# A hybrid decoder step: the sums of squares placed among product groups, w_o's parts spread one to a step, and silu(z) loaded behind a later chunk's operands

## The chip, the core and the metric

The kernel runs on one core of a Trainium2 chip. The core has five engines, each with its own instruction stream that it works through in order: PE (TensorE, the matrix multiplications and transposes), DVE (VectorE), ACT (ScalarE), POOL (GpSimd) and SP (SyncE, which here only issues DMA transfers). Engines wait for each other, and for transfers, by semaphores. An instruction that waits holds up everything behind it on its own engine; this goes for a DMA issue on SP too. Matrix results go to PSUM banks, all else lies in SBUF, and large arrays in the chip's memory. The metric is the device time of one execution in microseconds (us); lower is better.

## What is computed

One layer, for a prompt of 1024 tokens and for 8 samples of 8 tokens, with 1024 model channels; together 1088 columns of work. Cut to what matters here:

```
h = rmsnorm(x) * (1 + scale) + shift
[u_pool | z_pool | z_ssm | xBC | dt | g] = h @ w_in
P = (pool_mix(u_pool) * silu(z_pool)) @ w_pool_out
y = SSD(conv(xBC)) + D * x                      # a scan over chunks of 128 tokens, in 4 groups of 8 heads
S = (rmsnorm(y * silu(z_ssm)) * g) @ w_ssm_out  # the mean of squares runs over all 2048 channels
x = x + gate * ((sigmoid(g_pool) * P + sigmoid(g_ssm) * S) @ w_o)
out = rmsnorm(x)
```

Inside the scan, for each chunk and head: decay matrices `exp(...)` from the cumulated dt, an inner product of C and B weighted with them, the state carried from chunk to chunk, and at the end `v = (y + D x) * silu(z)`. The norm's factor 1/sqrt(mean(v*v)) is the same for all channels of a token, so the kernel multiplies v by w_ssm_out first and applies the factor afterwards. For it the squares of v are summed over the channels in `sq_acc`, 128 partitions by 1088 columns.

## The kernel before, in words

Everything is kept with channels on partitions and tokens along the free axis. Products are made in float32r from a high half (a rounded copy, on ACT) and a low half (the rest, by a subtraction on DVE or POOL), three matrix multiplications for a full product. The program has four stretches: the norm of x and the first projections; the projections with w_in, convolution and pooling; from about 795 us on the scan over chunks with product groups of w_pool_out and w_ssm_out between; and the last group's products, the gates, and the product with w_o.

The change is in the third stretch and at its seam to the fourth.

**The loop over chunks.** There are 32 chunks, 8 to each of the 4 groups. `chunk(g, c)` is a generator; the loop advances several of them in each iteration i, so that the work on chunk i stands beside the preparation of those behind it. Step 1 (called for chunk i+3 in iteration i) issues on SP the loads of `dec` (decays, 512 KB, three buffers), `bc` (128 KB, three buffers) and `xb` (256 KB, five buffers). Step 2 (for chunk i+2) makes the exponentials: POOL masks `dec` (L1294), ACT takes exp (L1298, L1603). Step 3 (chunk i+1) first loads `sz`, the 256 KB of silu(z) (L1609, three buffers), then transposes xb on PE (L1612) and prepares on DVE `xd`, `xw`, `dec`, `cE` (L1623 to L1632). Step 4 (chunk i) does the products of the scan on PE (L1637, L1310, L1313), updates the state `hst` (POOL L1643, DVE L1645) and adds D*x on DVE (L1650). Step 5 is `finish`: DVE multiplies by sz (L1570), ACT takes the high half and the square (L1572, L1573), POOL the low half (L1574, the last use of xb's buffer) and three additions that end in sq_acc (L1575 to L1581, the last use of sz's buffer).

**Product groups as fillers.** `pieces()` yields after each of 96 product groups (12 matrix multiplications into one of three PSUM banks, `mm`, which DVE or ACT then empties, L1831, L1849, L1852). `products(t)` advances it by 2.56 groups an iteration; ten are left after the loop.

**w_o.** `wo_splits()` makes five combinations of the quarters of w_o for a Strassen-like product, each in a high and a low half, and puts them into memory. It takes four passes, for 128 rows of each half of w_o: two loads of 512 KB (`R` from `in_w_o`, three buffers, L1895 and L1896), four operations on DVE (L1902 to L1908), then five parts, each a copy on ACT with its store from ACT's queue (`ph`, three buffers, L1883, L1884), a subtraction on POOL (L1885) and a store on SP (L1890). The loop advances it once an iteration from i = 10 on.

**What sets the order.** PE and SP issue in the order in which the code is written (`in_line`). On ACT, DVE and POOL a scheduler chooses the order when the program is built, so the place of an instruction in the code is not its place on these engines.

**The seam.** After the loop the ten product groups that are left come first. Then sq_acc is split into `sq_h` (ACT L1989) and `sq_l` (POOL L1991, written as `m`), six matrix multiplications with ones sum over the partitions (L1997, L1998), ACT takes the root (L1999) and DVE the reciprocal `rstd` in three pieces (L2000). The last group's products follow: eight units of three groups, each emptied by DVE (L2051), with four more operations of DVE per unit (L2044 with rstd, L2056, L2057, and L2032 or L2036).

Of the kernel before, what the change touches and what calls it, by code (L numbers as in the profile page):

```python
# [46 lines left out]
def tile_pool_ssd_step(  # L47
# [1535 lines left out]
    def sample_end(g):  # L1583
# [4 lines left out]
        yield  # L1588
        finish(g, SEQ, NS, v, sz)

    def chunk(g, c):
        o = c * P
        dec = ckt([P, 8, P], "dec", 3)
        decays(dec, g, c)
        bc = ckt([P, 2, P], "bc", 3)
        load(bc, xbc_d[g][:, 4:6, o:o + P])
        Bf, Cf = bc[:, 0], bc[:, 1]
        xb = ckt([P, 4, P], "xb", 5)
        load(xb, xbc_d[g][:, 0:4, o:o + P])
        yield  # L1600
        if c > 0:
            cE = ckt([P, 8, P], "cE")
            act(cE, dec, AF.Exp, scale=-1.0)  # L1603
        if g > 0 or c > 0:
            far(dec, c)
            exps(dec, g, c)
            yield
        sz = ckt([P, 4, P], "sz", 3)
        load(sz, z_d[g][:, :, o:o + P])  # L1609
        px = PB()  # L1610
        for q in range(4):
            nc.tensor.transpose(px[:, q * P:(q + 1) * P], xb[:, q], ident)  # L1612
# [10 lines left out]
        V.tensor_tensor(xd, pxv, dtT[:, c, heads].unsqueeze(2).to_broadcast([P, 8, 64]), ALU.mult)  # L1623
# [12 lines left out]
        pu = PC()  # L1636
        mm(pu, bt, xw.rearrange("p h d -> p (h d)"), start=True, stop=True)  # L1637
        pi = inner(xd, dec, P, *((hst[g], cE) if c > 0 else ()))
        hn = ckt([P, 512], "hst", 2)
        if c == 0:  # L1640
            act(hn, pu, AF.Copy)
        else:
            nc.gpsimd.tensor_tensor(hn.rearrange("p (h d) -> p h d", d=64), hst[g].rearrange("p (h d) -> p h d", d=64),  # L1643
                                    Elb[:, c, heads].unsqueeze(2).to_broadcast([P, 8, 64]), ALU.mult)
            V.tensor_tensor(hn, hn, pu, ALU.add)  # L1645
        hst[g] = hn

        v = xb
        for q in range(4):
            V.scalar_tensor_tensor(v[:, q], v[:, q], Dv[:, 4 * g + q:4 * g + q + 1], pi[:, q], ALU.mult, ALU.add)  # L1650
        yield
        finish(g, o, P, v, sz)
        if c == NC - 1:
            yield
            pt = PB()
            for q in range(4):
                nc.tensor.transpose(pt[:, q * P:(q + 1) * P], hn[:, q * P:(q + 1) * P], ident)
            fo = ckt([P, 4, P], "xb", 5)
            act(fo, pt.rearrange("p (q n) -> p q n", n=P), AF.Copy)
            store_(new_ssm_p[0, 0, 8 * g:8 * g + 8].rearrange("(q h) p n -> (h p) q n", h=2), fo)  # L1660
# [217 lines left out]
    def wo_splits():  # L1878
# [9 lines left out]
        def out():  # L1888
            while outs:
                load(*outs.pop(0))  # L1890
        left_, right_ = slice(0, 512), slice(512, 1024)

        def rows(k):
            up, dn = R(), R()
            load(up[:, :D], w_o[0, k * P:k * P + P, :])  # L1895
            load(dn[:, :D], w_o[0, 512 + k * P:512 + k * P + P, :])  # L1896
            return up, dn
        got = rows(0)
        yield
        for k in range(4):  # L1900
            up, dn = got
            WOE.tensor_tensor(dn[:, right_], dn[:, right_], up[:, right_], ALU.subtract)  # L1902
            WOE.tensor_tensor(up[:, right_], up[:, right_], up[:, left_], ALU.subtract)
            out()
            yield
            t2 = ckt([P, 512], "t2", 1)
            WOE.tensor_tensor(t2, dn[:, right_], up[:, left_], ALU.add)
            WOE.tensor_tensor(dn[:, left_], t2, dn[:, left_], ALU.subtract)  # L1908
            part(oT1, k, up[:, right_])
            yield  # L1910
            out()
            part(oB11, k, up[:, left_])
            part(oT2, k, t2)
            yield
            out()
            part(oT4, k, dn[:, left_])
            yield
            if k < 3:
                got = rows(k + 1)
            out()  # L1920
            part(oT3, k, dn[:, right_])
            yield
        out()
        yield
    WOE = V
    wos = wo_splits()
    RATE = 2.56
    FRONT = 4

    def products(t):  # L1930

# [9 lines left out]
    for _ in range(FRONT - 1):  # L1941
        next(pc_)
    next(seq[0])
    next(seq[1])
    next(pc_)
    in_line(first_engines)
    order = tuple(mybir.EngineType[e] for e in ORDER)
    for i in range(len(seq)):
        if i + 1 < len(seq):
            next(seq[i + 1])  # L1950
        products(i + 0.4)
        if i > 0:
# [33 lines left out]


    sq_h = mp.tile([P, T], F32R, tag="sq_h", name="sq_h", bufs=1)
    act(sq_h, sq_acc, AF.Copy)  # L1989
    sq_l = M(dt=F32R)  # L1990
    nc.gpsimd.tensor_tensor(sq_l, sq_acc, sq_h.bitcast(F32), ALU.subtract)  # L1991
    ones_r = sm.tile([P, P], F32R, tag="stc", name=nm("ones_r"), bufs=4)
    act(ones_r, ones, AF.Copy)
    rstd = mp.tile([P, T], F32, tag="rstd", name="rstd", bufs=1)
    for o, n in GB:
        ps = PB()
        mm(ps[:, :n], ones_r, sq_h[:, o:o + n], start=True, stop=False)  # L1997
        mm(ps[:, :n], ones_r, sq_l[:, o:o + n], start=False, stop=True)  # L1998
        act(rstd[:, o:o + n], ps[:, :n], AF.Sqrt, bias=eps, scale=1.0 / DI)  # L1999
        V.reciprocal(rstd[:, o:o + n], rstd[:, o:o + n])  # L2000
# [320 lines left out]
```

## Time and profile before

| | |
|---|---|
| median of three runs | 1261.52 us (1261.42 to 1265.95) |
| the profiled execution | 1261.8 us, span of its instructions 1260.1 us |
| granted TensorE clock, mean over the span | 0.995 |
| PE, DVE, POOL, ACT busy | 98%, 77%, 57%, 53% |
| w_o loads, of all passes | 8 of 512 KB, on SP |

A row of the timeline gives start and duration in us, engine, line, operation, `out<-in`, shapes, and in brackets how long the engine was idle before and what ended it. `SPq` is SP issuing a DMA. In the list of waits the numbers are the total in us, how often, and the longest. In the windows they are the stretch, its length, busy time (and instructions) of PE, PE's weight loads, DVE, ACT and POOL, then the granted clock, the DMA share and GB/s. In the chain of waits a row gives start, duration and what the chain went through.

### The profile page before, as it was taken

What the parts mean: (1) busy time and instruction counts of PE and PEld (TensorE: products, weight loads), DVE (VectorE), ACT (ScalarE), POOL (GpSimd) and SP (SyncE); (2) the same over time, 40 slices, a digit from 0 to 9 for tenths busy, and PEclk for the clock granted to TensorE, in tenths of its full rate; (3) what the DMA queues carried; (4) which work ended last, traced back from release to release, by engine and by line L of the source; (5) the groups of instructions that cost most, each with busy time, mean ns of one, the idle gap of its engine ahead of it and who ended that gap; (6) DMA issues with size and microseconds to landing.
All of it is one profiled execution on the core that took longest, in us unless ns stands there. A gap on an engine that the chain in (4) does not pass through costs nothing.

```text
span 1260.1 us, 26422 instructions
## 1 busy us (share of the span) xinstructions
PE 1237.0 (98%) x9703; PEld 1158.3 (92%) x9703; DVE 970.3 (77%) x1685; ACT 673.2 (53%) x1545; POOL 722.6 (57%) x608
## 2 busy tenths in 40 slices
PE   9999999999999999999999999999999989999997
PEld 8889999999999999999999999998898978898885
DVE  6893888877988688886666675687787969679996
ACT  6764366655656566546444444556586646401425
POOL 1137768776968678654433435255677758513663
PEclk9999999999999999999999999999999989999999
DMA  9946455474546554435575665997869868775884
GB/s 317 309 137 212 124 177 178 135 233 129 184 154 202 164 154 159 157 111 152 158 199 162 179 195 171 329 312 256 261 221 312 259 215 259 242 268 186 251 194 157
DMA packets 262715, 257.53 MB, mean 204 GB/s; under 512 B 27993, under 2 KB 202345, under 8 KB 262578
## 3 DMA queue, kind: packets, MB, share of 16 engines
q1 hardware_dynamic: 181856, 163.49, 42.4%
q10 hardware_dynamic: 78426, 88.16, 20.2%
q0 software_dynamic: 2304, 4.20, 1.9%
q8 instruction: 77, 1.26, 0.4%
q14 instruction: 52, 0.43, 0.1%
HBM read 170.80 MB, written 85.10 MB: 203 GB/s over the span
## 4 chain that ended last, share of the span: by engine, by line
PE 62%; DVE 5%; DMA 3%; issue 1%; POOL 1%; ACT 0%; SPq 0%; DVEq 0%; ACTq 0%; POOLq 0%
PE mm L427 14%; PE ps L427 14%; PE mm L235 13%; PE ps L1310 2%; PE pc L427 2%; PE pc L1637 2%; PE ps L1313 2%; PE ps L2118 2%; PE ps L2116 2%; PE ps L2117 2%; DMA R<-in_w_o 1%; PE ps L1402 1%; DMA xb<-xbc 1%; PE ps L1612 1%; PE ps L1425 1%
## 5 line engine op out<-in xcount | busy, mean ns | idle before, releaser
L151 POOL TENSOR_TENSOR wlo<-rawA,whi 128x512 fp32r<-128x512 f32 x120 | 173.1, 1446 | 115.9 <-ACT whi L148 105.6
L151 POOL TENSOR_TENSOR wlo<-raw,whi 128x512 fp32r<-128x512 f32 x90 | 152.8, 1707 | 89.4 <-ACT whi L148 85.3
L235 PE MATMUL mm<-Y,whi 128*128 128x352 f32 (+1 forms) x960 | 198.0, 336 | 2.7 <-DVE G L2051 2.2
L235 PEld LDWEIGHTS mm<-Y,whi 128*128 128x128 f32 x960 | 160.0, 189 | 11.0 <-DVE G L2051 4.9
L1148 DVE SCALAR_TENSOR_TENSOR GA<-GA,cvT,GA 128x1112 f32<-128x1112 f32 x72 | 133.8, 1863 | 0.1
L427 PE MATMUL mm<-Y,whi 128*128 128x272 f32 x800 | 120.1, 292 | 0.0
L148 ACT ACTIVATE whi<-rawA 128x512 fp32r<-128x512 f32 x120 | 75.2, 627 | 82.6 <-PE ps L427 45.6
L427 PE MATMUL ps<-Y,whi 128*128 128x272 f32 x800 | 117.8, 289 | 0.0
L427 PEld LDWEIGHTS mm<-Y,whi 128*128 128x128 f32 x800 | 107.6, 188 | 2.6 <-issue 1.1
L148 ACT ACTIVATE whi<-raw 128x512 fp32r<-128x512 f32 x90 | 55.8, 628 | 100.9 <-DVE raw L364 42.4
L427 PEld LDWEIGHTS ps<-Y,whi 128*128 128x128 f32 x800 | 106.7, 188 | 0.3
L235 PE MATMUL mm<-Y,wlo 128*128 128x352 f32 (+1 forms) x480 | 99.0, 328 | 0.0
L1298 ACT ACTIVATE dec<-dec,acT 128x128 f32<-128x128 f32 x256 | 78.5, 389 | 25.1 <-POOL dec L1294 25.1
L235 PEld LDWEIGHTS mm<-Y,wlo 128*128 128x128 f32 x480 | 82.2, 189 | 0.0
L302 POOL TENSOR_TENSOR pw<-pw,ph 128x512 fp32r<-128x512 f32 x40 | 66.5, 1663 | 10.5 <-ACT ph L300 10.2
L427 PE MATMUL mm<-G,whi 128*128 128x272 f32 x480 | 71.0, 290 | 0.0
L427 PE MATMUL ps<-G,whi 128*128 128x272 f32 x480 | 70.5, 289 | 0.0
L427 PE MATMUL mm<-Y,wlo 128*128 128x272 f32 x400 | 66.7, 288 | 0.0
L427 PE MATMUL ps<-Y,wlo 128*128 128x272 f32 x400 | 66.5, 288 | 0.0
L1574 POOL TENSOR_TENSOR Y<-xb,Y 128x512 fp32r<-128x512 f32 x32 | 41.2, 1290 | 42.0 <-ACT Y L1572 42.0
L427 PEld LDWEIGHTS mm<-G,whi 128*128 128x128 f32 x480 | 64.4, 189 | 0.7
L427 PEld LDWEIGHTS ps<-G,whi 128*128 128x128 f32 x480 | 64.2, 188 | 0.4 <-issue 0.4
(597 smaller groups left out, 3260.0 us busy)
## 6 DMA issues: line engine op xcount, KB each, us to landing
rawA<-in_w_in SPq DMA_DIRECT2D x62, 512.0 KB
dec<-acs_d SPq DMA_DIRECT2D x32, 512.0 KB
xbc<-GA ACTq DMA_DIRECT2D x24, 512.0 KB
Y<-wo SPq DMA_DIRECT2D x10, 1024.0 KB
pw<-in_w_ssm_out ACTq DMA_DIRECT2D x32, 256.0 KB
ws<-ph ACTq DMA_DIRECT2D x32, 256.0 KB
ws<-pw ACTq DMA_DIRECT2D x32, 256.0 KB
h<-in_state_ssm SPq DMA_DIRECT2D x32, 256.0 KB
```

What stands on the lines that cost most here:

```text
L148: ins = act(hi[:, :, :ncols], raw[:, :, :ncols], AF.Copy)
L151: (eng or nc.gpsimd).tensor_tensor(lo[:, :, :ncols], raw[:, :, :ncols], hi[:, :, :ncols].bitcast(F32), ALU.subtract)
L235: mm(ps[:, :n], w[k // 4][h][:, k % 4, :], r[k][:, o:o + n], start=(j == 0), stop=(j == len(terms) - 1))
L302: nc.gpsimd.tensor_tensor(raw.bitcast(F32R), raw, hi.bitcast(F32), ALU.subtract)
L427: mm(p, w[j // 8][:, k], A(k, s)[j // 4 == 1], start=(j == 0), stop=(j == 11))
L1148: V.scalar_tensor_tensor(d[:, :n], rp[:, k:k + n], cvT[:, 24 * k + mc:24 * k + mc + 1], d[:, :n], ALU.mult, ALU.add)
L1298: act(dec[:, h], dec[:, h], AF.Exp, bias=acT[:, c, 8 * g + h:8 * g + h + 1], scale=-1.0)
L1310: mm(o[hh], xd[:S, 2 * q + hh, :], dec[:S, 2 * q + hh], start=True, stop=state is None)
L1313: mm(o[hh], state[:, h * 64:h * 64 + 64], cE[:, h], start=False, stop=True)
L1574: nc.gpsimd.tensor_tensor(yl[g][:, :, o:o + S], v, yhc.bitcast(F32), ALU.subtract)
L1637: mm(pu, bt, xw.rearrange("p h d -> p (h d)"), start=True, stop=True)
L2116: mm(ps, hi, y[:, k, c0:c0 + cw], start=(first and k == 0), stop=False)
```

## The change

Three things are moved; the arithmetic is the same.

- sz is no longer loaded in step 3 of its chunk. `load_sz(j)` loads it, called in iteration i for chunk i+1, after step 1 of chunk i+3.
- `wo_splits()` starts at i = 8 and loads one 512 KB block at a time; each step holds one part at most.
- After the loop only four of the ten product groups come first. sq_h and sq_l are made in three pieces each, sq_l on DVE. Each sum over the partitions is followed by its root, reciprocals of at most 128 columns (nine in all) and one product group; the last three groups come behind.

```diff
+    szs = []
+
+    def load_sz(j):
+        g, c = divmod(j, NC)
+        szs.append(ckt([P, 4, P], "sz", 3))
+        load(szs[-1], z_d[g][:, :, c * P:c * P + P])
+
     def chunk(g, c):
...
-        sz = ckt([P, 4, P], "sz", 3)
-        load(sz, z_d[g][:, :, o:o + P])
         px = PB()
...
-        finish(g, o, P, v, sz)
+        finish(g, o, P, v, szs.pop(0))
...
-        def rows(k):
-            up, dn = R(), R()
-            load(up[:, :D], w_o[0, k * P:k * P + P, :])
-            load(dn[:, :D], w_o[0, 512 + k * P:512 + k * P + P, :])
-            return up, dn
-        got = rows(0)
+        def row(o):
+            t = R()
+            load(t[:, :D], w_o[0, o:o + P, :])
+            return t
+        up, dn = row(0), None
         yield
         for k in range(4):
-            up, dn = got
-            WOE.tensor_tensor(dn[:, right_], dn[:, right_], up[:, right_], ALU.subtract)
-            WOE.tensor_tensor(up[:, right_], up[:, right_], up[:, left_], ALU.subtract)
             out()
+            if k:
+                part(oT3, k - 1, dn[:, right_])
+            old, dn = dn, row(512 + k * P)
+            yield
+            V.tensor_tensor(dn[:, right_], dn[:, right_], up[:, right_], ALU.subtract)
+            V.tensor_tensor(up[:, right_], up[:, right_], up[:, left_], ALU.subtract)
+            out()
+            if k:
+                part(oT4, k - 1, old[:, left_])
             yield
             t2 = ckt([P, 512], "t2", 1)
-            WOE.tensor_tensor(t2, dn[:, right_], up[:, left_], ALU.add)
-            WOE.tensor_tensor(dn[:, left_], t2, dn[:, left_], ALU.subtract)
+            V.tensor_tensor(t2, dn[:, right_], up[:, left_], ALU.add)
+            out()
             part(oT1, k, up[:, right_])
             yield
+            V.tensor_tensor(dn[:, left_], t2, dn[:, left_], ALU.subtract)
             out()
             part(oB11, k, up[:, left_])
-            part(oT2, k, t2)
             yield
             out()
-            part(oT4, k, dn[:, left_])
-            yield
+            part(oT2, k, t2)
             if k < 3:
-                got = rows(k + 1)
-            out()
-            part(oT3, k, dn[:, right_])
+                up = row(k * P + P)
             yield
...
+    BEFORE = 4
...
     next(seq[0])
+    load_sz(0)
     next(seq[1])
...
             next(seq[i + 3])
+        if i + 1 < len(seq):
+            load_sz(i + 1)
         if i + 2 < len(seq):
             next(seq[i + 2])
         next(seq[i], None)
...
-        if i > 9:
+        if i > 7:
             next(wos, None)
         products(i + 1.0)
     next(seq[-1], None)
-    for it in (pc_, wos):
-        for _ in it:
-            pass
-    in_line(order)
+    for _ in wos:
+        pass
+    for _ in range(BEFORE):
+        next(pc_)
...
     sq_h = mp.tile([P, T], F32R, tag="sq_h", name="sq_h", bufs=1)
-    act(sq_h, sq_acc, AF.Copy)
     sq_l = M(dt=F32R)
-    nc.gpsimd.tensor_tensor(sq_l, sq_acc, sq_h.bitcast(F32), ALU.subtract)
...
+    for o, n in GB:
+        s = slice(o, o + n)
+        act(sq_h[:, s], sq_acc[:, s], AF.Copy)
+        V.tensor_tensor(sq_l[:, s], sq_acc[:, s], sq_h[:, s].bitcast(F32), ALU.subtract)
     for o, n in GB:
...
         act(rstd[:, o:o + n], ps[:, :n], AF.Sqrt, bias=eps, scale=1.0 / DI)
-        V.reciprocal(rstd[:, o:o + n], rstd[:, o:o + n])
+        for a in range(o, o + n, P):
+            b = min(a + P, o + n)
+            V.reciprocal(rstd[:, a:b], rstd[:, a:b])
+        next(pc_, None)
+    for _ in pc_:
+        pass
+    in_line(order)
```

The lines behind the change shift by up to 23, so the loop's L1609 is L1596 afterwards, L1885 is L1890, L1902 is L1910 and L2000 is L2019. What the change does to the engines' orders is shown at three places.

SP, from the loads of chunk 25 (the first three rows) to those of chunk 26, before. The sz is that of chunk 24:

```order
L1290 DMA dec_13976<-acs_d 128x1024
L1596 DMA bc_13978<-xbc_173 128x2x128
L1599 DMA xb_13980<-xbc_173 128x4x128
L1609 DMA sz_14021<-z_169 128x4x128
L324 DMA whi_14038<-ws_201 128x512
L325 DMA wlo_14039<-ws_201 128x512
L1290 DMA dec_14082<-acs_d 128x1024
L1596 DMA bc_14084<-xbc_173 128x2x128
L1599 DMA xb_14086<-xbc_173 128x4x128
```

The same stretch now, where sz_13986 is that of chunk 23 and sz_14091 that of chunk 24:

```order
L1290 DMA dec_13980<-acs_d 128x1024
L1603 DMA bc_13982<-xbc_173 128x2x128
L1606 DMA xb_13984<-xbc_173 128x4x128
L1596 DMA sz_13986<-z_168 128x4x128
L1895 DMA wo_11259<-R_13542 128x512
L324 DMA whi_14041<-ws_201 128x512
L325 DMA wlo_14042<-ws_201 128x512
L1290 DMA dec_14085<-acs_d 128x1024
L1603 DMA bc_14087<-xbc_173 128x2x128
L1606 DMA xb_14089<-xbc_173 128x4x128
L1596 DMA sz_14091<-z_169 128x4x128
```

sz of chunk 24 has moved from ahead of chunk 26's three loads to behind them.

DVE in w_o's third pass, before (`R` and `t` are w_o's, `hst`, `xb`, `xd`, `xw`, `dec` and `cE` the chunks', `G<-mm` a product bank being emptied):

```order
L1625 TENSOR_TENSOR xw_13812<-ps_13799,wdT 128x512
L1645 TENSOR_TENSOR hst_13849<-hst_13849,pc_13830 128x512
L1630 TENSOR_TENSOR dec_13614<-dec_13614,ps_13804 128x1024
L1632 TENSOR_TENSOR cE_13743<-cE_13743,ps_13804 128x1024
L1902 TENSOR_TENSOR R_13771<-R_13771,R_13770 128x512
L1650 SCALAR_TENSOR_TENSOR xb_13510<-xb_13510,Dv,ps_13832 128x128 x4
L1852 TENSOR_TENSOR G_12637<-mm_13885,G_12637 128x352
L1903 TENSOR_TENSOR R_13770<-R_13770 128x512
L1907 TENSOR_TENSOR t_2351_14000<-R_13771,R_13770 128x512
```

And now:

```order
L1628 TENSOR_TENSOR xd_13693<-ps_13682,dtT 128x512
L1910 TENSOR_TENSOR R_13648<-R_13648,R_13542 128x512
L1857 TENSOR_TENSOR G_12513<-mm_13699,G_12513 128x352
L1635 TENSOR_TENSOR dec_13509<-dec_13509,ps_13687 128x1024
L1637 TENSOR_TENSOR cE_13623<-cE_13623,ps_13687 128x1024
L1911 TENSOR_TENSOR R_13542<-R_13542 128x512
L1917 TENSOR_TENSOR t_2334_13884<-R_13648,R_13542 128x512
L1630 TENSOR_TENSOR xw_13695<-ps_13682,wdT 128x512
L1650 TENSOR_TENSOR hst_13732<-hst_13732,pc_13713 128x512
```

Before, w_o's operations came behind xw and hst of a chunk; now they come one chunk earlier (chunk 21 in place of 22), and xw and hst stand behind three of them.

POOL in the same pass now (`R` and `t` with `ph` are w_o's five subtractions):

```order
L1294 AFFINE_SELECT dec_13615<-dec_13615 128x1024
L1890 TENSOR_TENSOR R_13542<-R_13542,ph_13887 128x512
L1890 TENSOR_TENSOR R_13542<-R_13542,ph_14008 128x512
L1648 TENSOR_TENSOR hst_13849<-hst_13732,Elb 128x512
L1890 TENSOR_TENSOR t_2334_13884<-t_2334_13884,ph_14114 128x512
L1890 TENSOR_TENSOR R_13648<-R_13648,ph_14239 128x512
L1574 TENSOR_TENSOR Y_13240<-xb_13386,Y_13239 128x4x128
L1575 TENSOR_TENSOR sz_13621<-sz_13621 128x256
L1294 AFFINE_SELECT dec_13739<-dec_13739 128x1024
L1890 TENSOR_TENSOR R_13648<-R_13648,ph_14365 128x512
```

Before, the five stood within eight instructions of POOL, with hst, Y and sz between the third and the fourth; now they stand within nine. The code's steps are one part long, but the order of POOL is the scheduler's.

DVE at the seam, before and now:

```order
L1852 TENSOR_TENSOR G_13216<-mm_15126,G_13216 128x384
L1852 TENSOR_TENSOR G_13216<-mm_15140,G_13216 128x352
L1852 TENSOR_TENSOR G_13216<-mm_15154,G_13216 128x352
L2000 RECIPROCAL rstd<-rstd 128x384
L2000 RECIPROCAL rstd<-rstd 128x352 x2
L2051 TENSOR_TENSOR G_12255<-mm_15223,G_12255 128x384
```

```order
L1857 TENSOR_TENSOR G_12953<-mm_15070,G_12953 128x352
L2019 RECIPROCAL rstd<-rstd 128x128 x3
L1857 TENSOR_TENSOR G_13076<-mm_15109,G_13076 128x384
L2019 RECIPROCAL rstd<-rstd 128x128 x2
L2019 RECIPROCAL rstd<-rstd 128x96
L1857 TENSOR_TENSOR G_13076<-mm_15130,G_13076 128x352
L2019 RECIPROCAL rstd<-rstd 128x128 x2
L2019 RECIPROCAL rstd<-rstd 128x96
L1857 TENSOR_TENSOR G_13076<-mm_15151,G_13076 128x352
L1857 TENSOR_TENSOR G_13216<-mm_15165,G_13216 128x384
L2067 TENSOR_TENSOR R_15228<-rstd,R_15228 128x1088
```

The reciprocals have moved from ahead of the last group's first eviction to between the evictions of the product groups ahead of it.

More of the change, by code (lines that the diff above doesn't have):

```diff
@@ L1891, in wo_splits @@
         left_, right_ = slice(0, 512), slice(512, 1024)
-        def rows(k):
-            up, dn = R(), R()
-            load(up[:, :D], w_o[0, k * P:k * P + P, :])
-            load(dn[:, :D], w_o[0, 512 + k * P:512 + k * P + P, :])
-            return up, dn
-        got = rows(0)
+        def row(o):
[3 more added lines that the diff above has]
+        up, dn = row(0), None
         yield
         for k in range(4):
-            up, dn = got
-            WOE.tensor_tensor(dn[:, right_], dn[:, right_], up[:, right_], ALU.subtract)
-            WOE.tensor_tensor(up[:, right_], up[:, right_], up[:, left_], ALU.subtract)
             out()
+            if k:
[7 more added lines that the diff above has]
+                part(oT4, k - 1, old[:, left_])
             yield
             t2 = ckt([P, 512], "t2", 1)
-            WOE.tensor_tensor(t2, dn[:, right_], up[:, left_], ALU.add)
-            WOE.tensor_tensor(dn[:, left_], t2, dn[:, left_], ALU.subtract)
+            V.tensor_tensor(t2, dn[:, right_], up[:, left_], ALU.add)
+            out()
             part(oT1, k, up[:, right_])
             yield
+            V.tensor_tensor(dn[:, left_], t2, dn[:, left_], ALU.subtract)
             out()
             part(oB11, k, up[:, left_])
-            part(oT2, k, t2)
             yield
             out()
-            part(oT4, k, dn[:, left_])
-            yield
+            part(oT2, k, t2)
             if k < 3:
-                got = rows(k + 1)
-            out()
-            part(oT3, k, dn[:, right_])
+                up = row(k * P + P)
             yield
         out()
+        part(oT3, 3, dn[:, right_])
         yield
-    WOE = V
+        out()
+        part(oT4, 3, dn[:, left_])
+        yield
+        out()
     wos = wo_splits()
```

## The prediction

> **What bounds the kernel now.** I read the page's busy times first, then who waited for whom on PE, then the chain of waits, and last the rows of SP, POOL, DVE and PE around each wait. The page:
>
> ```profile
> PE 1237.0 (98%) x9703; PEld 1158.3 (92%) x9703; DVE 970.3 (77%) x1685; ACT 673.2 (53%) x1545; POOL 722.6 (57%) x608
> ```
>
> PE is busy nearly always, so only its idle and its slow time can be won. The waits of PE, one wait of SP, and three windows tell where these lie:
>
> ```profile
> PE ps L1612 <- DMA xb<-xbc: 5.7, 2, 4.6
> PE mm L235 <- DVE G L2051: 2.2, 3, 1.5
> ...
> PE ps L1313 <- POOL Y L1574: 0.7, 1, 0.7
> ```
> ```profile
> SPq L1609 <- POOL sq_acc L1581: 29.9, 7, 9.0
> ```
> ```profile
> 1000.00:1020.00 20.00, 19.24 (x152) 16.54 (x150) 18.04 (x31) 13.31 (x36) 18.66 (x19) 1.00 0.46 136
> ...
> 1028.00:1030.00 2.00, 1.90 (x9) 1.93 (x10) 0.69 (x1) 0.94 (x4) 1.03 (x1) 0.50 1.11 391
> ```
>
> Two groups of transposes waited for xb, 4.63 and 1.05 us. After the first the granted clock is 0.50 for a while. The chain of waits shows what that cost, beside the same work at full clock:
>
> ```profile
> 1012.13 4.04 PE mm L235 x24
> 1016.17 0.44 PE ps L1612 x4
> ...
> 1020.93 7.04 DMA xb<-xbc
> ...
> 1028.10 1.09 PE ps L1612 x4
> ...
> 1029.83 5.60 PE mm L235 x24
> ```
>
> 24 products took 5.60 in place of 4.04 and four transposes 1.09 in place of 0.44: 2.2 us on top of the 4.63. The large stall costs 6.8 us, the small one 1.05.
>
> Why xb came late: SP's rows, then POOL's.
>
> ```profile
> 1003.21 0.33 SPq L1290 DMA_DIRECT2D dec<-acs_d  x1
> ...
> 1004.07 0.51 SPq L1599 DMA_DIRECT2D xb<-xbc  x1
> 1018.26 0.53 SPq L1609 DMA_DIRECT2D sz<-z  x1
> ...
> 1020.93 0.46 SPq L1599 DMA_DIRECT2D xb<-xbc  x1
> ...
> 1068.49 0.53 SPq L1609 DMA_DIRECT2D sz<-z  x1
> ...
> 1070.21 0.46 SPq L1599 DMA_DIRECT2D xb<-xbc  x1
> ```
> ```profile
> 999.64 0.89 POOL L1581 TENSOR_TENSOR sq_acc<-sq_acc,sz 128x128 f32<-128x128 f32 x1
> ...
> 1002.75 2.99 POOL L1885 TENSOR_TENSOR R<-R,ph 128x512 fp32r<-128x512 f32 x2 [0.72 <-ACT ph L1883]
> ...
> 1009.08 1.27 POOL L1574 TENSOR_TENSOR Y<-xb,Y 128x512 fp32r<-128x512 f32 x1
> ...
> 1017.77 0.88 POOL L1581 TENSOR_TENSOR sq_acc<-sq_acc,sz 128x128 f32<-128x128 f32 x2
> ...
> 1065.60 1.30 POOL L1574 TENSOR_TENSOR Y<-xb,Y 128x512 fp32r<-128x512 f32 x1
> ...
> 1067.99 0.47 POOL L1581 TENSOR_TENSOR sq_acc<-sq_acc,sz 128x128 f32<-128x128 f32 x1
> ```
>
> SP goes in order. (I number the 32 chunks from 0 on through the four groups.) From 1004.6 to 1018.26 it stood at sz of chunk 24, until POOL had added chunk 21 to sq_acc, which is when that buffer of sz comes free; POOL was late there, with w_o's subtractions (L1885) in a bunch before it. Behind this sz stood dec, bc and xb of chunk 26. The same happened with sz of chunk 29 (chunk 26 added at 1068.46) and xb of chunk 31.
>
> **The change, part by part.** *sz behind the loads.* No load is added. Now xb of chunk i+3 stands ahead of sz of chunk i+1; the sz ahead of it is that of chunk i, which needs POOL one chunk less far. For xb 26 that is sz 23, free once chunk 20 was added: 999.64 + 0.89 = 1000.5. What is left for xb is PE, which holds dec's buffer, and POOL's L1574, which holds xb's own. PE's rows:
>
> ```profile
> 1000.44 1.02 PE L1637 MATMUL pc<-xw,bt 128*128 128x512 f32 x2
> ...
> 1008.16 1.02 PE L1637 MATMUL pc<-xw,bt 128*128 128x512 f32 x2
> ...
> 1028.10 1.09 PE L1612 MATMUL ps<-ident,xb 128*128 128x128 f32 x4 [4.63 <-DMA xb<-xbc]
> ...
> 1060.22 1.02 PE L1637 MATMUL pc<-xw,bt 128*128 128x512 f32 x2
> ...
> 1075.95 0.66 PE L1612 MATMUL ps<-ident,xb 128*128 128x128 f32 x4 [1.05 <-DMA xb<-xbc]
> ```
>
> dec is loaded 2.8 us after L1637 (1000.44 and 1003.21), xb 0.9 later. One chunk on, L1637 at 1008.16 gives xb 26 at 1011.9, its L1574 having ended at 1010.35. With the measured 7.04 it lands at 1018.9, and PE wanted it at 1028.10 - 4.63 = 1023.5: covered by 4.6 us. For xb 31, L1637 at 1060.22 gives 1063.9, but its L1574 ends at 1066.9; with 7.04 it lands at 1073.9 and is wanted at 1074.9: covered by 1.0 us. So both stalls go: 6.8 + 1.05 = 7.85 us. Bounds: 0, where another late thing takes their place, and 7.85. What that 0.50 clock makes of a stall that only shrinks is told by a page: the Trainium skill, TensorE: Matmul & The Clock Gate, What's actually happening, says that the clock halves after an idle window of about 3.4 us. The trace agrees (0.50 after 4.63 us, no slower products after 1.05). By that rule a stall left at 2 us would still give back all 2.2 us of slow clock, and the sum would be 2 us worse, not 2.9.
>
> What is late next is sz itself. Chunk 24's could still not go before 1018.26; by xb's 7.04 it lands at 1025.3, and DVE multiplied by it at
>
> ```profile
> 1025.92 0.68 DVE L1570 TENSOR_TENSOR xb<-xb,sz 128x512 f32<-128x512 f32 x1
> ```
>
> so it is just in time in the worst chunk. I take 0; the other end is 2 us, once, if it lands as late as xb's longest wait suggests.
>
> *w_o's parts.* The same eight loads, 16 DVE operations, 20 halves on ACT and POOL and 40 stores; the first load two chunks earlier, one 512 KB block at a time in place of two. In the new program's order POOL's five subtractions of a pass still stand within ten instructions (shown with the change), so the spreading itself I cost at nothing. What can cost is DVE, which waited for w_o before:
>
> ```profile
> DVE R L1902 <- DMA R<-in_w_o: 5.6, 3, 3.8
> ```
> ```profile
> 987.69 7.23 DMA R<-in_w_o
> ```
> ```profile
> L1903 DVE TENSOR_TENSOR R<-R x4: 677/687/1515, 907.8 to 1050.0; 128x512 f32<-128x512 f32 x4
> ```
>
> The second block of a pass is now issued behind sz and one store, about half a us later after its dec than before, and lands 7.2 us after. In the third pass the first subtraction stands right behind xd of chunk 21, and xw of chunk 21 stands behind three of w_o's operations. In this trace these places are
>
> ```profile
> 976.11 0.34 SPq L1290 DMA_DIRECT2D dec<-acs_d  x1
> ```
> ```profile
> 982.78 0.68 DVE L1623 TENSOR_TENSOR xd<-ps,dtT 128x512 f32<-128x512 f32 x1
> ```
> ```profile
> 990.80 1.02 PE L1637 MATMUL pc<-xw,bt 128*128 128x512 f32 x2
> ```
>
> so the block goes at about 976.1 + 2.4 = 978.5 and lands at 985.7; DVE is there at 983.4 and waits 2.3 us. Then seven operations (four of 0.6 to 0.7, two of dec and cE at 1.2, an eviction of 0.5) bring xw to 991.3, 0.5 us after PE wanted it. In the other passes the next consumer on PE stands a chunk further on. I take a loss of 0.5; bounds 0 and 2.4 us in each pass. The rule that speaks against this part is in the Trainium skill, SBUF — State Buffer, Who interferes with whom: a DVE instruction with two SBUF inputs and a POOL instruction that reads SBUF shut each other out for a whole instruction. The 677 to 1515 ns of L1903 agree. By that rule all three operations of w_o ahead of xw would be held, to about 1.5 us each, xw would be 3.0 us late in place of 0.5, and the forecast would stand at 1255.0. The 0.7 us of L1313 is of the same kind; I leave it standing.
>
> *Sums of squares and reciprocals.* The rows at the seam between the loop and the last group's products:
>
> ```profile
> 1097.26 0.56 DVE L1852 TENSOR_TENSOR G<-mm,G 128x384 f32<-128x384 f32 x1 [1.55 <-PE mm L235]
> ...
> 1113.90 6.98 DVE L2000 RECIPROCAL rstd<-rstd 128x384 f32<-128x384 f32 x3 [0.44 <-ACT rstd L1999]
> ...
> 1122.06 3.68 DVE L2044 TENSOR_TENSOR R<-rstd,R 128x1088 f32<-128x1088 f32 x3
> ```
> ```profile
> 1121.34 0.97 PE L235 MATMUL mm<-Y,whi 128*128 128x384 f32 x4 [1.52 <-DVE G L2051]
> ```
>
> From 1093 to 1113 DVE does one eviction of about 0.5 us for each product group of PE, 1.95 us, and is idle in between. Then 6.98 us of reciprocals stand ahead of the evictions, and PE pays 2.2 us in three waits. The change puts 7 us of reciprocals, the 3.7 of L2044 and three subtractions of 0.5 (the low half, now DVE's) beside the same ten product groups. Six of them, 11.7 us, come behind the first sum; their evictions need 3.2, the reciprocals and L2044 10.7: DVE enters the last group about 2.2 us behind instead of 7 and then 3.7. A piece of 128 columns takes a third of the 2.3 to 2.6 us of a reciprocal, 0.85, so no eviction waits long, and PE's lead of three banks, two groups or 3.9 us, hides the rest. The four groups ahead of the first sum last from 1093 to 1100.9, POOL's last addition ends at 1096.4, so ACT's three pieces and DVE's subtractions are covered by 4.5 us. I take 1.7 of the 2.2 us, since L2056 and L2057 keep DVE nearly full behind it; bounds 0 and 2.2.
>
> **Sum.** 7.85 + 1.7 - 0.5 = 9.05 us off the profiled execution's 1261.8: 1252.7. The median of the three runs is 0.3 lower (1261.52); rounded down, 1252.5.
>
> **Rivals.** *DVE stands at w_o's second block (the slower side).* If the longest wait seen, 3.8 us, comes in all four passes and DVE's next three operations take 1.5 in place of 0.68 (+2.5), DVE is 6.3 us late in each. Where a product bank is PE's next need, its lead of 3.9 us leaves 2.4 to pay; where xw is, nothing covers. At a mean of 4.5 us in a pass 18 are lost and 9.55 won: 1270. It decides from 2.4 us a pass on. For it: DVE's 18.04 of 20 us busy from 1000 on. Against it: it waited in three passes before, and PE lost 0.7.
>
> *Another late thing takes half the stall.* POOL was busy 18.66 of those 20 us, DVE 18.04, and the stall let both catch up; without it the next chunk may wait for cE or hst instead. Half of the 6.8 is then kept: about 1256.
>
> *The move of sz does nothing:* POOL's L1574 is so late that xb waits for it as sz did. The 1.0 us of xb 31 speaks for it, the 4.6 of xb 26 against. Only the seam is won: 1260.
>
> **Chances.** My forecast 0.60, half the stall 0.20, only the seam 0.08, slower 0.12. A measurement of this kernel can tell about 0.5%, 6.3 us, from no change, so faster means below 1255.2. The forecast and two fifths of the second case lie there: 0.68 faster, 0.20 within, 0.12 slower. The range goes from 1250, where 7.85 + 0.7 + 2.2 are won, to 1262, which takes in all but the slower case.
>
> **What would show it.** Right: no wait of PE for xb and no clock of 0.50 in the chunk loop; SP's wait for sq_acc still there, with dec and xb issued ahead of it; reciprocals between evictions and no wait of 1.5 us behind them. Wrong: PE waiting for DVE or POOL between two chunks, DVE waiting for w_o more than 3.8 us in a pass, or L1570 waiting for sz.

## The result, and the profile after

The changed kernel takes 1252.68 us (median of 6 executions, 1248.57 to 1254.32). The kernel before, with three more executions beside it, has a median of 1264.58 us (1261.42 to 1265.95). The ratio is 0.9907, 95% interval 0.9886 to 0.9928. The two profiled executions are 7.5 us apart (spans of 1260.1 and 1252.6 us); one state product early and one late cut both into three stretches. Line numbers have moved: the state product is L1637 before and L1642 after, silu(z)'s load L1609 and L1596, xb's load L1599 and L1606. PE's first and last state products in the timeline of the kernel after:

```profile
810.51 1.02 PE L1642 MATMUL pc<-xw,bt 128*128 128x512 f32 x2
...
1083.31 1.02 PE L1642 MATMUL pc<-xw,bt 128*128 128x512 f32 x2
```

Before, these rows began at 809.48 and 1087.74. So the way to the first state product is 1.0 us longer (of the edits only the first loads of silu(z) lie there, and a second execution of the same kernel was 1.1 us shorter there than before), the chunk loop takes 272.8 us in place of 278.3 (5.5 less), and the rest, from the last state product to the end, 169.3 in place of 172.4 (3.1 less). These three lengths are given for every run below; the first varies from 808.1 to 811.2 us among all of them, whatever the edit.

The loop first. SP's rows and POOL's rows for the same chunks as in the prediction:

```profile
1005.72 0.44 SPq L1606 DMA_DIRECT2D xb<-xbc  x1
1008.06 0.52 SPq L1596 DMA_DIRECT2D sz<-z  x1
...
1013.43 0.42 SPq L1606 DMA_DIRECT2D xb<-xbc  x1
1013.94 0.53 SPq L1596 DMA_DIRECT2D sz<-z  x1
```
```profile
1007.57 0.47 POOL L1581 TENSOR_TENSOR sq_acc<-sq_acc,sz 128x128 f32<-128x128 f32 x1
...
1011.49 0.46 POOL L1581 TENSOR_TENSOR sq_acc<-sq_acc,sz 128x128 f32<-128x128 f32 x1
```

The first sz still goes out right behind an addition to sq_acc (1007.57 + 0.47, then 1008.06), but xb stands ahead of it. Where SP stood for 13.7 us before, the longest pause between two of its rows from 950 us on is 7.6 us, and it is not at silu(z). The waits of SP and of PE from 780 us on:

```profile
SPq L1596 <- POOL sq_acc L1581: 12.6, 5, 4.5
```
```profile
PE ps L1310 <- DVE cE L1637: 1.8, 1, 1.8
PE ps L1310 <- ACT dec L1298: 1.2, 1, 1.2
PE ps L1619 <- DMA dec<-acs_d: 0.4, 1, 0.4
PE mm L235 <- DVE Y L1680: 0.3, 1, 0.3
```

No wait for xb is left. In their place stand two waits that the kernel before did not have, 1.8 and 1.2 us. The timelines of DVE, SP, PE and ACT show where they come from:

```profile
1040.77 0.67 DVE L1650 TENSOR_TENSOR hst<-hst,pc 128x512 f32<-128x512 f32 x1
1045.05 1.26 DVE L1570 TENSOR_TENSOR v<-v,szs 128x256 f32<-128x256 f32 x1 [3.61 <-DMA v<-ys]
1046.23 1.21 DVE L1635 TENSOR_TENSOR dec<-dec,ps 128x1024 f32<-128x1024 f32 x1
1047.36 1.21 DVE L1637 TENSOR_TENSOR cE<-cE,ps 128x1024 f32<-128x1024 f32 x1
```
```profile
1037.82 1.49 SPq L1587 DMA_DIRECT2D v<-ys  x1
```
```profile
1048.72 0.44 PE L1310 MATMUL ps<-dec,xd 128*64 128x128 f32 x4 [1.82 <-DVE cE L1637]
...
1058.02 0.44 PE L1310 MATMUL ps<-dec,xd 128*64 128x128 f32 x4 [1.18 <-ACT dec L1298]
```
```profile
1051.42 0.63 ACT L1572 ACTIVATE Y<-xb 128x512 fp32r<-128x512 f32 x1 [2.89 <-DVE xb L1570]
...
1052.98 2.43 ACT L1298 ACTIVATE dec<-dec,acT 128x128 f32<-128x128 f32 x8
```
```profile
1055.52 1.22 DVE L1635 TENSOR_TENSOR dec<-dec,ps 128x1024 f32<-128x1024 f32 x1 [1.48 <-ACT dec L1298]
1056.66 1.21 DVE L1637 TENSOR_TENSOR cE<-cE,ps 128x1024 f32<-128x1024 f32 x1
```

v holds the sample columns of the last group; they are multiplied by their silu(z) (tile szs) once a group. The load goes out at 1037.82 and lands 7.2 us later; DVE reaches the multiplication at 1041.4 and stands 3.6 us, and dec and cE of the next chunk, which PE's next products need, stand behind it. That is the wait of 1.8 us. The second follows from it one chunk on: ACT waited 2.9 us for the late DVE, its exponentials came behind that, and DVE waited 1.5 us for these before its next dec and cE. The profile names ACT for this wait of PE, but PE starts 0.15 us after cE ends, as it did at the first. In the kernel before the same multiplication stood behind dec and cE, and its load had 9.4 us:

```profile
1042.84 0.87 SPq L1587 DMA_DIRECT2D v<-ys  x1
```
```profile
1047.77 1.21 DVE L1630 TENSOR_TENSOR dec<-dec,ps 128x1024 f32<-128x1024 f32 x1
1048.90 1.21 DVE L1632 TENSOR_TENSOR cE<-cE,ps 128x1024 f32<-128x1024 f32 x1
...
1052.27 0.76 DVE L1570 TENSOR_TENSOR v<-v,szs 128x256 f32<-128x256 f32 x1
```

The edit does not touch that multiplication. The scheduler, which orders DVE, put it elsewhere; that it did so because other work had moved is a reading of the orders and was not tested. The stand is 3.1 to 3.9 us in the three executions that have both w_o's edit and the move of sz's load, with v's load where it was. It is 0.7 and 0.8 us in the two that have w_o's edit without sz's move, and absent in the two that have sz's move without w_o's edit.

The seam. DVE's rows after the first sum, and PE's waits from 1083 us on:

```profile
1097.63 2.58 DVE L2019 RECIPROCAL rstd<-rstd 128x128 f32<-128x128 f32 x3 [0.44 <-ACT rstd L2016]
1100.13 0.49 DVE L1857 TENSOR_TENSOR G<-mm,G 128x384 f32<-128x384 f32 x1
1100.54 2.36 DVE L2019 RECIPROCAL rstd<-rstd 128x128 f32<-128x128 f32 x3
...
1106.31 3.69 DVE L2067 TENSOR_TENSOR R<-rstd,R 128x1088 f32<-128x1088 f32 x3
```
```profile
PE mm L235 <- DVE G L2074: 0.9, 1, 0.9
```

The nine reciprocals and the products with rstd lie between evictions, DVE is done with them at 1110, and one wait of 0.9 us in the last group is left of the 2.2.

### The profile page after: what moved, and what is told of

It reads as the page before. It is cut to its first block, busy times and chain, and to the rows that moved or that the text cites. A ratio compares the mean times of both kernels' runs of the same rounds, so it can differ in the third digit from the quotient of the medians.

```text
span 1252.6 us, 26438 instructions
## 1 busy us (share of the span) xinstructions
PE 1232.8 (98%) x9703; PEld 1155.4 (92%) x9703; DVE 968.5 (77%) x1694; ACT 673.3 (54%) x1547; POOL 716.6 (57%) x607
## 4 chain that ended last, share of the span: by engine, by line
PE 65%; DVE 4%; DMA 2%; issue 1%; SPq 1%; POOL 0%; ACT 0%; DVEq 0%; ACTq 0%; POOLq 0%
PE mm L235 16%; PE mm L427 14%; PE ps L427 14%; PE ps L1310 3%; PE pc L427 2%; PE pc L1642 2%; PE ps L1313 2%; PE ps L2139 2%; PE ps L2141 2%; PE ps L2140 2%; PE ps L1402 1%; PE ps L1617 1%; PE ps L1425 1%; PE pc L1416 1%; DMA dec<-acs_d 1%
## 5 line engine op out<-in xcount | busy, mean ns | idle before, releaser
L151 POOL TENSOR_TENSOR wlo<-rawA,whi 128x512 fp32r<-128x512 f32 x120 | 172.5, 1442 | 114.2 <-ACT whi L148 98.9
```

What stands on the lines that cost most here:

```text
L151: (eng or nc.gpsimd).tensor_tensor(lo[:, :, :ncols], raw[:, :, :ncols], hi[:, :, :ncols].bitcast(F32), ALU.subtract)
```

## The experiments

Each run is compared with executions of the kernel before on the same chip. "Loop" is the way from the first state product to the last, "rest" that from there to the end, each from the run's one profiled execution.

| run | ratio (95% interval) | loop us | rest us | PE's largest wait in the loop, us |
|---|---|---|---|---|
| before | 1 | 278.3 | 172.4 | 4.6, xb |
| whole change | 0.9907 (0.9886 to 0.9928) | 272.8 | 169.3 | 1.8, cE |
| whole change again | 0.9916 (0.9900 to 0.9932) | 273.6 | 169.3 | 1.6, cE |
| silu(z) alone | 0.9937 (0.9921 to 0.9954) | 271.4 | 173.6 | 1.2, ACT's xb |
| w_o alone | 0.9955 (0.9944 to 0.9966) | 273.4 | 172.7 | 1.1, cE |
| seam alone | 0.9977 (0.9968 to 0.9986) | 278.3 | 169.3 | 5.1, xb |
| w_o and seam | 0.9922 (0.9910 to 0.9934) | 274.2 | 169.3 | 1.6, cE |
| silu(z) and seam | 0.9903 (0.9887 to 0.9918) | 272.5 | 169.4 | 1.9, ACT's xb |
| w_o earlier, not spread | 0.9947 (0.9933 to 0.9961) | 272.7 | 172.6 | 1.9, cE |
| w_o spread, not earlier | 0.9949 (0.9933 to 0.9965) | 271.2 | 172.4 | 1.0, xw |
| before without POOL's subtractions | 0.9936 (0.9920 to 0.9952) | 270.4 | 172.5 | 0.9, cE |
| whole change, v earlier | 0.9904 (0.9891 to 0.9918) | 269.8 | 169.3 | 0.7, cE |
| silu(z), seam, v earlier | 0.9916 (0.9898 to 0.9934) | 270.9 | 169.3 | 1.3, ACT's xb |
| whole change, three reciprocals | 0.9907 (0.9894 to 0.9921) | 271.4 | 169.5 | 1.2, dec |

Runs in which the code of the loop is the same differ in its length: 272.8, 273.6 and 271.4 us (the whole change, twice, and with three reciprocals), 271.4 and 272.5 (the load moved), 273.4 and 274.2 (w_o's edit). So loops that are 1 or 2 us apart are not told apart.

**The parts one by one.** The kernel before with the load alone:

```
+        if i + 1 < len(seq):
+            load_sz(i + 1)          # behind next(seq[i + 3])
...
-        sz = ckt([P, 4, P], "sz", 3)
-        load(sz, z_d[g][:, :, o:o + P])
```

> The kernel before with the load of silu(z) alone moved behind the loads of the row three ahead. If that load's place is what held xb (the forecast's reason), both waits of PE for xb and the half clock go: 7.85 us, ratio about 0.994. If instead the new spreading of w_o's parts cured POOL's lateness and the load's place does nothing, PE still waits about 4.6 us for xb and the ratio is 0.998 to 1.000.

Measured 0.9937, loop 271.4 us: 6.9 us of the 7.85 are won, and no wait for xb is left. POOL's, SP's and PE's rows for chunk 26's xb:

```profile
1017.71 0.88 POOL L1581 TENSOR_TENSOR sq_acc<-sq_acc,sz 128x128 f32<-128x128 f32 x2
```
```profile
1015.53 0.42 SPq L1606 DMA_DIRECT2D xb<-xbc  x1
1018.20 0.52 SPq L1596 DMA_DIRECT2D sz<-z  x1
```
```profile
1023.25 0.60 PE L1617 MATMUL ps<-ident,xb 128*128 128x128 f32 x4
```

POOL is as late as before (1017.71 beside 1017.77), but xb no longer stands behind it: it goes at 1015.53 in place of 1020.93, and PE's transposes come without a wait. The forecast's reason holds for this part by itself. (Its rest is 1.3 us longer than before's; PE waited 3.0 us for DVE's evictions in place of 2.2, so the old seam is not even as short each time.)

The kernel before with w_o alone (the new body of `wo_splits` and):

```
-        if i > 9:
+        if i > 7:
             next(wos, None)
```

> The kernel before with w_o's parts alone spread, one block and one part a step, from two chunks earlier. The forecast's reason: POOL's subtractions still stand close together, SP still stands at silu(z) and PE still waits for xb; DVE's waits for w_o cost about 0.5 us: ratio about 1.000, and 0.999 to 1.002. Rival: the spreading takes POOL's bunch away and with it the wait for xb: 5 to 8 us won, ratio 0.994 to 0.996.

Measured 0.9955, loop 273.4 us: 4.9 us won. The forecast's number for it, 1.000, is wrong. SP still stands at silu(z), 30.2 us in all, but the longest stand comes far earlier in the loop. SP's timeline, and what PE waited for from 780 to 1100 us:

```profile
908.22 0.46 SPq L1599 DMA_DIRECT2D xb<-xbc  x1
920.36 0.53 SPq L1609 DMA_DIRECT2D sz<-z  x1
```
```profile
PE ps L1310 <- DVE cE L1632: 1.1, 1, 1.1
PE ps L1612 <- DMA xb<-xbc: 1.0, 1, 1.0
```

A stand of 11.7 us at 908 us cost 1.0 us of PE; one of 13.7 at 1004 us cost 4.6 and the half clock. So about 9 us of a stand (13.7 less 4.6) to 11 us (11.7 less 1.0) are free, since xb is loaded three chunks ahead.

The kernel before with the seam alone (the hunks of the diff with `BEFORE`, `sq_l` and the reciprocals):

> The kernel before with the sums of squares and the nine reciprocals alone moved in among the last products. Forecast's term: 1.7 us won, ratio 0.9987, waits of PE for DVE in the last group down from 2.2 to about 0.5 us. The trace of the changed kernel shows 3.4 us less from the loop's end to the last instruction: by that reading the ratio is 0.997.

Measured 0.9977: loop 278.3 us as before, rest 169.3 us, 3.1 less. The size of the forecast was too small, for a reason that the profile of before had shown; the view of waits from 1087 to 1177 us has a row for PE's weight loads, and the same view of the kernel after has the second row:

```profile
PEld mm L235 <- DVE G L2051: 4.9, 8, 1.8
```
```profile
PEld mm L235 <- DVE G L2074: 1.2, 1, 1.2
```

In these traces the weight load carries the wait for an eviction. 4.9 us in eight waits became 1.2 in one, 3.7 us less; the rows of PE itself, 2.2 and 0.9, counted only what was left once the matmul ahead had ended by the model. The weight loads' rows are not an exact price either: with the load alone they have 4.6 us, and the rest is 1.3 us longer than before's.

The whole change with the load back in its old place:

> The changed kernel with the load of silu(z) back in its old place, w_o's parts and the seam as changed. If the load's place is the cause: SP stands at silu(z) again, PE waits for xb, and only the seam is won: ratio 0.997 to 0.999. If w_o's spreading is the cause: no wait for xb, ratio 0.991 as for the whole change.

Measured 0.9922, loop 274.2 us, no wait for xb. The rival's number, not the forecast's: with the load moved or not, the stall is gone. Both edits cure the same stall, and either is enough. (SP still stood 11.3 us at silu(z), at 907 us, and no wait of PE for xb followed; w_o alone had 11.7 us there and 1.0 us of PE.) That raises two questions: what the spreading does beside the load's move, and by what it cures.

**Is w_o's part needed?** The whole change with w_o as before:

> The changed kernel with w_o's parts as before: the load of silu(z) and the seam alone. If the load's move and the spreading of w_o both cure the same stall and the second brings nothing more, the chunk loop takes 271.4 us as with the load's move alone, the rest 169.3 us as with the seam alone: 6.9 + 3.1 = 10 us won, ratio 0.992, no worse than the whole change. If the two add up, it is 2 to 5 us behind the whole change: ratio 0.993 to 0.995.

Measured 0.9903, beside 0.9907 and 0.9916 of the whole change: w_o's part adds nothing that can be measured to the other two. The loop came out at 272.5 us, not at the 271.4 expected, a difference that loops of the same code show. One wait is larger than with the load alone (1.9 against 1.2 us):

```profile
PE ps L1619 <- ACT xb L1664: 1.9, 1, 1.9
```

L1664 is ACT's copy of a group's last state, at the end of the third group; PE's next transposes need the bank that it frees.

**Earlier, or spread?** w_o's part does two things, and each was run alone on the kernel before: the start two chunks earlier (`i > 7`, old body), and one part a step (new body, `i > 9`).

> The kernel before with w_o's work begun two chunks earlier and nothing else: the five subtractions of a pass in the same bunch on POOL. If it is the chunk on which the bunch falls that makes xb late, the wait for xb at chunk 25 goes from 4.6 us to under 1.5 us and the ratio is 0.995 to 0.997, as with the spreading; a wait of that size at another chunk would say that the bunch is late wherever it falls. If it is the spreading over more steps that cures, the wait of over 3.5 us stays or moves to another chunk: ratio 0.999 to 1.001.

> The kernel before with w_o's parts one a step, begun in the same chunk as before. If only the chunk on which the bunch falls counts, a wait of PE for xb of 3 us or more is still there and the ratio is 0.998 to 1.000. If the spreading cures on its own, no wait for xb over 1.5 us and a ratio of 0.994 to 0.996.

Measured 0.9947 and 0.9949: each alone cures, and no wait for xb is left in either. So the cure needs neither the one nor the other, and each must do something that both have in common. POOL's timelines, first spread but not earlier, then earlier but not spread:

```profile
1007.29 0.95 POOL L1581 TENSOR_TENSOR sq_acc<-sq_acc,sz 128x128 f32<-128x128 f32 x1
1010.59 2.52 POOL L1885 TENSOR_TENSOR R<-R,ph 128x512 fp32r<-128x512 f32 x2
1013.07 1.73 POOL L1885 TENSOR_TENSOR t<-t,ph 128x512 fp32r<-128x512 f32 x1
1015.81 2.55 POOL L1885 TENSOR_TENSOR R<-R,ph 128x512 fp32r<-128x512 f32 x2
```
```profile
980.90 0.90 POOL L1581 TENSOR_TENSOR sq_acc<-sq_acc,sz 128x128 f32<-128x128 f32 x1
982.23 2.54 POOL L1885 TENSOR_TENSOR R<-R,ph 128x512 fp32r<-128x512 f32 x2 [0.43 <-ACT ph L1883]
985.78 1.27 POOL L1885 TENSOR_TENSOR t<-t,ph 128x512 fp32r<-128x512 f32 x1 [1.00 <-ACT ph L1883]
...
990.27 2.56 POOL L1885 TENSOR_TENSOR R<-R,ph 128x512 fp32r<-128x512 f32 x2
995.71 0.46 POOL L1581 TENSOR_TENSOR sq_acc<-sq_acc,sz 128x128 f32<-128x128 f32 x1
```

In both the five subtractions of the pass are a bunch still, 6.8 and 6.4 us of work within 7.8 and 10.6 us. What differs is where the bunch falls among the additions to sq_acc. Before, it ran from 1002.75 to 1013.54 and the addition of chunk 21, behind all of it, came at 1017.77. Spread, the addition that frees the next sz stands ahead of the bunch; earlier, the additions on both sides of the bunch are 14 us apart and SP's longest stand at sz between 950 us and the end is 7.3 us. The bunch made this stall in one position, and either edit moves it out of that position. It can hold up an addition elsewhere too: with both edits, spread and earlier (the run with w_o alone), the first pass's five subtractions lie from 900.6 to 912.6 us, the next addition that frees an sz ends at 920.34, and that is the stand of 11.7 us, most of which was covered.

The last link was tried by itself: the kernel before without POOL's subtractions.

```
             store_(wo_d[o][:, 0, k], hi.bitcast(F32))
-            nc.gpsimd.tensor_tensor(t.bitcast(F32R), t, hi.bitcast(F32), ALU.subtract)
             outs.append((wo_d[o][:, 1, k], t))
```

> The kernel before with POOL's twenty subtractions of w_o left out (the low halves are not formed: what is stored in their place is the full number, so the products with w_o come out wrong; no transfer, no other operation and no wait on DMA is changed). If POOL's bunch is what makes the addition to sq_acc late, and SP's stand at silu(z) and xb's lateness follow from it, SP never stands over 10 us at silu(z) from 950 us on, neither wait of PE for xb is left, and the way from the first to the last state product falls from 278.3 to 270 to 271.5 us: ratio 0.993 to 0.995. If POOL is late for another reason (its own finish work, or ACT ahead of it), the wait of 4.6 us stays: ratio 0.999 to 1.000.

Measured 0.9936, loop 270.4 us, no wait of PE for xb; from 950 us on SP's longest stand at silu(z) is 5.8 us. Load, spreading, earlier start and less work on POOL each remove the same stall; that SP stood at silu(z) for POOL, with xb queued behind, is shown from both ends.

**The load of v.** The whole change with v and its silu(z) loaded one chunk earlier:

```
-        if i % NC == 2:
+        if i % NC == 1:
             ends = sample_end(i // NC)
             next(ends)
```

> The changed kernel with the loads of the sample column's v and silu(z) issued one chunk earlier (in the third chunk's place of a group the second). In the changed kernel DVE stands 3.6 us at the multiplication of v in the last group, with dec and cE of the next chunk behind it, and PE waits 1.8 and then 1.2 us for those. If that load is the cause, the way from the state product of chunk 0 to that of chunk 31 falls from 272.8 to about 269.8 us and the ratio to about 0.988. If POOL or ACT is late there anyway, the waits come back under another name: 272 to 273 us, ratio 0.9905.

The loop takes 269.8 us as expected, the shortest of all, and the waits of 1.8 and 1.2 us are gone; PE's largest in the loop is

```profile
PE ps L1313 <- DVE cE L1637: 0.7, 1, 0.7
```

The ratio, 0.9904 and not the 0.988 expected, is not told apart from the whole change's 0.9907 and 0.9916: 3 us are 0.24%, and the intervals are 0.27 to 0.42% wide. So the trace shows the stall and its cure, and the times do not show the gain. Whether the wait was one execution's was asked of the changed kernel itself:

> The changed kernel once more, beside its variants. The first profile had 272.8 us from the first to the last state product, with waits of PE of 1.8 and 1.2 us behind the load of v; the variant with whole reciprocals, which leaves the loop as it is, had 271.4. If the wait for v is there in every execution, 271 to 273 us; if it was one execution's, about 269.8. Ratio 0.989 to 0.992.

Loop 273.6 us, with waits of 1.6, 1.2 and 0.8 us and DVE again 3.9 us at v: it is there in both. The remaining combination:

> The changed kernel with w_o's parts as before and the loads of v one chunk earlier: the load of silu(z), the seam and v. If w_o's spreading is not needed and the two waits are independent, no wait of PE in the loop over 1.9 us, 271 to 272.5 us from the first to the last state product and ratio 0.989 to 0.991. If v's load in its new place stands in front of something xb needs, a wait for xb or dec comes back: 0.992 or more.

Measured 0.9916, loop 270.9 us, both just outside what was expected, on opposite sides; the largest wait is 1.3 us, for ACT's copy of the state. No version here beats the whole change by more than can be told; the shortest of its kind in the trace is the whole change with v earlier.

**Nine pieces or three.**

> The changed kernel with three reciprocals of 384, 352 and 352 columns in place of nine of 128 or less, in the same places among the products. If the place is what counts, the way from the last state product to the end stays at 169.3 us and the ratio at 0.9905. If the pieces count, an eviction stands 2.3 to 2.6 us behind a reciprocal, weight loads of PE wait for DVE by 0.5 us or more at the seam, and it is 0.5 to 2 us longer: ratio 0.991 to 0.992.

Measured 0.9907, rest 169.5 us. The weight loads' wait for DVE is even smaller than with nine pieces:

```profile
PEld mm L235 <- DVE G L2072: 0.5, 1, 0.5
```

Cutting the reciprocals small adds nothing; the 3.1 us come from the rest of the seam's edit, the place among the products with sq_l in pieces on DVE. Of these two the place is the likely one, but sq_l's part was not run by itself.

## Why the prediction was right or wrong

The forecast was 1252.5 us and the median is 1252.68. That is closer than its terms deserve: the profiled execution gained 7.5 us against 9.05 forecast, and the median of before moved up by 3.1 us with more executions. In the profile the loop fell 1.9 us short of the forecast's 7.35 (7.85 less 0.5), the rest went 1.4 us beyond its 1.7, and the way to the first state product took 1.0 more. That the medians meet to 0.2 us is luck; the forecast's two main terms are right in cause and off in size.

- *Both stalls of xb go, 7.85 us.* Right for the changed kernel and for the load alone (6.9 us of the loop). xb was expected 3.7 us behind the state product of the chunk; PE's row at 1009.79 and SP's at 1013.43 are 3.6 us apart. With the load alone the distance is 7.0 us (1008.49 and 1015.53), since bc stood 3.2 us behind dec; with the 7.04 us of the transfer xb then lands at about 1022.6, 0.7 us before PE's transposes and not 4.6.
- *"The spreading itself I cost at nothing."* This is the step that failed. I had read that the five subtractions stay close together, which is so, and took it that POOL stays late. Alone it wins 7.1 us of the loop, the earlier start alone 5.6, both 4.9, which are not told apart among each other. The sum was not hurt, since the load's move had already been credited with the same 7.85 us; the gain belongs to either edit, and the change holds two cures for one stall.
- *DVE waits for w_o, 0.5 us lost.* Forecast: a wait of 2.3 us in the third pass. Measured: 4.6 us in four waits, the longest 2.1, that in the third pass. No wait of PE followed, so the term is 0 here. That rests on the scheduler's order: in the third pass of the changed kernel DVE does dec and cE ahead of L1911 and L1917, while with w_o alone and with w_o and seam it does three of w_o's operations ahead of them, and PE waits 1.0 and 1.6 us for cE at 990 us. The slower rival at 1270 us did not come near: it needed 2.4 us a pass lost on PE.
- *sz in time.* DVE waited 0.9 us once for sz, at no cost to PE.
- *The rival "another late thing takes half the stall".* It came in part: 3.4 us of 8.55 (xb's 7.85 and the 0.7 of L1313, which went too) returned as waits for cE and dec. I had named cE; I put it on POOL and DVE being full, and 3.0 of the 3.4 came from one load, v's, that I had not listed among the things that move. I costed the operations that the diff moves, not those that the scheduler moves because of it.
- *The seam, 1.7 us in bounds of 0 to 2.2.* Mis-sized: 3.1 us. The upper bound came from PE's rows and left out the 4.9 us of the weight loads' row. The reason (DVE free between evictions) was right; the argument about pieces was not needed. Beside the load's move the seam is worth more, 4.3 us (173.6 with the load alone, 169.4 with load and seam).
- *The clock.* The prediction weighed a sentence of the Trainium skill, TensorE: Matmul & The Clock Gate, What's actually happening: an idle window of about 3.4 us halves the clock. The runs agree from both sides. With the seam alone the wait for xb was 5.1 us, and the window of 5 us behind it has a granted clock of 0.62:

```profile
1029.80 1.09 PE L1612 MATMUL ps<-ident,xb 128*128 128x128 f32 x4 [5.12 <-DMA xb<-xbc]
```
```profile
1030.00:1035.00 5.00, 5.00 (x23) 5.00 (x23) 1.13 (x2) 3.29 (x11) 1.68 (x3) 0.62 1.08 384
```

In the runs whose longest wait is 1.9 us or less it stayed at 1.00 through the loop, in windows of 5 us. No run left a stall between 1.9 and 4.6 us, so where between them the clock falls is not shown.
- *The rule on DVE and POOL* (the Trainium skill, SBUF — State Buffer, Who interferes with whom). The run without POOL's subtractions bears on it. w_o's last operation on DVE, two inputs in SBUF, in the groups by line, before and without the subtractions:

```profile
L1908 DVE TENSOR_TENSOR R<-t,R 128x512 f32<-128x512 f32 x4 | 4.3, 1072 | 0.0
```
```profile
L1907 DVE TENSOR_TENSOR R<-t,R 128x512 f32<-128x512 f32 x4 | 2.7, 679 | 0.0
```

The same operation takes 1072 ns on average with them in the program and 679 without; of the three long ones of the four, two lay beside a subtraction and one beside POOL's work on hst. Of the other three, two also got shorter (892 to 786, 748 to 680), and one got longer (951 to 1052), with POOL's remaining work beside it. The rival that the forecast drew from this, three operations of about 1.5 us each ahead of xw, did not come: in the changed kernel's third pass they took 1.20, 0.68 and 0.68 us. It did not decide the time here.

## What to carry to other kernels

When an in-order queue stands for a buffer, look for everything that could move the release: here four separate edits removed the same 5 to 8 us, so their gains do not add, and an edit costed at nothing may be a second cure for a stall that another edit has been credited with. Read the waits of the weight loads beside those of the products: they held 4.9 us where the products' rows showed 2.2. Where a scheduler orders some engines, list also the instructions that the edit does not name but that change places, and ask of each whether its load is early enough.

## What the runs showed that was not expected

- The three stretches of this program repeat very differently. The rest after the loop came out at 169.26 to 169.35 us in all seven runs that have the seam as changed, and the unedited loop at 278.26 and 278.31, but the edited loops vary by up to 2.2 us at the same code, and the way to the first state product, where the edits move next to nothing, by 3.1 us. A gain of 3 us can be seen in the trace of a stretch and not in the total.
- A full reciprocal of 352 to 384 columns costs DVE the same 2.3 to 2.6 us as three pieces of it (2.55 and 2.34 us in the run with three, 2.58 and 2.36 with nine), and PE's products cover one of that length: the rest is 169.5 us with three and 169.3 with nine.
